# x transposed by channel tiles of four token tiles, with its loads and the weights' placed between the quarters of w_mod

## The chip, the cores and the metric

The kernel runs on one core of a Trainium2 chip. The core has five engines, each with its own queue that it works off in order: TensorE (PE, matrix products and transposes; its weight loads are shown apart as PEld), VectorE (DVE), ScalarE (ACT), GpSimd (POOL) and SyncE (SP, which here issues the DMAs). PE writes to PSUM, eight banks of 128 x 512 fp32 values; DVE and ACT read PSUM and the on-chip memory. Time is device microseconds (us) of one execution. Before the change: 1352.6 us, the median of three runs (1351.03 to 1353.95).

## What is computed

One layer of a diffusion transformer on 1024 latent tokens of width 1024, all in fp32: adaptive RMSNorm, one wide projection, windowed attention beside Fourier mixing, a gated merge, and a gated feed-forward with a short convolution. The part that matters here is the beginning, the modulated norm of x and the projection:

```python
def adaln(cvec, w_mod, b_mod):
    return jnp.split(jax.nn.silu(cvec) @ w_mod + b_mod, 6, axis=-1)
...
sh1, sc1, gt1, sh2, sc2, gt2 = [m[:, None] for m in adaln(c, w_mod[l], b_mod[l])]
...
h = modulate(rmsnorm(x, g_pre1[l]), sh1, sc1)
hc = modulate(rmsnorm(ctx, g_pre1[l]), csh1, csc1)
q, k, v, f, g_a, g_f = split_proj(h @ w_in[l])
```

`modulate(h, shift, scale)` is `h * (1 + scale) + shift`, one scale and one shift per channel. w_mod has 1024 rows and 6 x 1024 columns; the first 2048 columns give shift and scale of this norm, the other 4096 the four vectors needed later.

## The kernel before

**Precision.** A product of fp32 matrices is made of three products of a narrower type (`mm3`): each operand is split into a high part (a cast, on ACT) and a low part (source minus high part, on DVE); `split` does both. A matmul of 512 columns is issued three times, lines 85, 86 and 87.

**The projection.** h, transposed so that channels lie on the partitions, is the moving operand. It is cut in four: token half 1 or 2 by channel half 1 or 2, each of 4 channel tiles of 128 by 512 tokens: B11, B21, B12, B22. A Strassen-Winograd scheme (`wino`) multiplies a pair of column blocks of w_in with 7 products instead of 8: P1 to P7, with the operands B11, B21, B22 and the differences T1, T2, T3, T4n of the four pieces (`MOV`), and on the weights' side A11, A12, A22 and the sums S1 to S4 (`STA`). The first three pairs (j = 0 to 2: three pairs of gate columns) run in a hand-written order; items 0-2 are P1 of the three, 3-5 P2, 6-8 P5, 9-11 P6, 12-14 P7, 15 and 16 P4 and P3 of pair 0. `mm(i, ks)` issues the matmuls of item i for the channel tiles `ks` (all four: 12 matmuls), `conv(j, p)` splits the weight operand, `sums(j, s)` makes a sum on DVE, `evac(i)` copies or adds a result out of PSUM. One bank per pair holds P1, P6, P7 and P4 (X), one P5 and P3 (Y), one P2 (Z).

**The vectors.** The first 2048 columns of w_mod come in four quarters (`wm_stage(q)`, 8 loads of 256 KB each; quarter q holds shift and scale of channel tiles 2q and 2q + 1). `mod_rows(q, ks)` multiplies them with silu(c), `mod_copy` (DVE) takes the rows out of PSUM, `mod_turn` (PE, 8 tiny matmuls) turns them into columns, `mod_vec` (DVE) makes the scale `ax` and the shift `sx`. The other 4096 columns follow in groups of 512 (`ada_load`, `ada_rows`, `ada_copy`).

**x.** Eight token tiles of 128 tokens, each loaded as two halves of 512 channels (`x_load`). `x_square` sums squares on ACT, `x_norm` makes 1/rms of two tiles, `x_scale` scales. Then, for one token tile and one channel half, PE transposes four 128 x 128 blocks into one PSUM bank (`transpose8`, `turn`): the bank holds four channel tiles of one token tile. Scale and shift differ between channel tiles, so `affine` takes each block of 128 columns by itself, on ACT or DVE (`x_first` from PSUM; `x_second` from a raw copy, `x_raw`, for channel half 2 of the first four tiles). The splits (`hb_part`, `hb_puts`) go by token tile, too: pieces of 128 to 384 columns, since the operand lies in one buffer of 3 channel tiles and one of 1. The differences T1 to T4n are made per token tile over 512 columns.

**Order.** In the block under `tc.manual_schedule()` (from line 899) each engine runs its instructions in the order of the text. All loads of the block come first in it, so SP's queue starts with x tiles 0-3, the four quarters with A11 between the second and third, then the rest. `mm(3)` follows the split of B21, `mm(6)` that of T1, `mm(9)` that of T2, `mm(12)` that of T3, item 15 needs T4n and item 16 B22. From item 17 on `run` issues the items with their loads, splits and evacuations a fixed number of items ahead.

Of the kernel before, what the change touches and what calls it, by code (L numbers as in the profile page):

```python
# [13 lines left out]
ALU = mybir.AluOpType  # L14
# [26 lines left out]
def block_kernel(ctx: ExitStack, tc: tile.TileContext, t: dict, out: bass.AP, dbg: dict):  # L41
# [18 lines left out]
    def s(name, dtype=F):  # L60
        return spool.tile([P, 512], dtype, tag="s", name=name, bufs=40)
# [92 lines left out]
    def transpose8(xn, psf, name):  # L154

        res = []
        for kh in range(2):
            pt = psf(f"pt{name}{kh}")
            for k in range(4):
                nc.tensor.transpose(pt[:, k * P:(k + 1) * P], xn[kh][:, k * P:(k + 1) * P], ident)  # L160
            res.append(pt)
        return res
# [375 lines left out]
    def affine(out, src, kh, eng, ks):  # L538
        for k in ks:
            a, b = ax[:, 0, kh * 4 + k:kh * 4 + k + 1], sx[:, 0, kh * 4 + k:kh * 4 + k + 1]  # L540
            o, i = out[:, k * P:(k + 1) * P], src[:, k * P:(k + 1) * P]
            if eng is None:
                nc.scalar.activation(out=o, in_=i, func=AF.Identity, scale=a, bias=b)
            else:
                eng.tensor_scalar(out=o, in0=i, scalar1=a, scalar2=b, op0=ALU.mult, op1=ALU.add)

    def x_turn(tk):
        pt[tk] = transpose8(xs[tk], ps, f"x{tk}")
# [3 lines left out]
    def x_raw(tk):  # L552

        hraw[tk, 1] = s(f"hr{tk}1")
        copy(hraw[tk, 1], pt[tk][1])
# [343 lines left out]
    with tc.manual_schedule():  # L899
        for tk in range(4):  # L900
# [12 lines left out]
        pre(1, ("A12",))  # L913
# [12 lines left out]
        for tk in range(2):  # L926
            for i in range(2):
                x_scale(tk, i, nc.vector)
        x_turn(0)
        x_turn(1)  # L930
        x_norm(2)
        mod_rows(0, range(4))
        for tk in range(2, 4):
            for i in range(2):
                x_scale(tk, i, nc.vector)
        x_raw(0)
        x_raw(1)
        x_turn(2)
        x_turn(3)
        x_raw(2)  # L940
        x_raw(3)
# [24 lines left out]
        mod_rows(2, range(8))
        ada_load(1, range(KT))
        mm(0, range(2, 4))
        mod_copy(2)
        mod_turn(2)  # L970
        mm(1, range(2, 4))
        mod_vec(2)
        engs = (nc.vector, None, None, nc.vector)
        b21 = {c: hraw[c, 1] for c in (0, 1, 3, 2)}
        for c in range(4):
            x_second(c, (0, 1), engs[c])
        mod_rows(3, range(4))
        mm(2, range(2, 4))
        mod_rows(3, range(4, 8))
        ada_load(2, range(KT))  # L980
        hb_part(hb, "B21", b21, 0, 2)
        conv(0, "P2")
        mod_copy(3)
        mod_turn(3)
        x_square(4)
        x_square(5)
        mod_vec(3)

        def turn(tk, kh):
            p_ = ps(f"ptx{tk}{kh}")  # L990
            for k in range(4):
                nc.tensor.transpose(p_[:, k * P:(k + 1) * P], xs[tk][kh][:, k * P:(k + 1) * P], ident)
            pt.setdefault(tk, {})[kh] = p_
# [24 lines left out]
        for tk in (6, 7):
            turn(tk, 0)
        for tk in (6, 7):  # L1020
            x_first(tk, range(4), 0, alt_(tk))
        mm(5)
        ada_rows(0, 1)
        for c in range(4):
            t1(c)
        sums(0, "S1")
        hb_puts(hb, "T1", {c: hraw[c, 0] for c in range(4)})
        conv(0, "P5")
        ada_copy(0)
        ada_load(3, range(KT))  # L1030
        for tk in range(4, 8):
            x_scale(tk, 1, None)
        ada_rows(1, 0)
        ada_rows(1, 1)
        ada_copy(1)
        ada_load(4, range(KT))
        for tk in (4, 5):
            turn(tk, 1)
        for j in range(3):
            evac(j)  # L1040
        for j in range(3, 6):
            evac(j, True)
        sums(1, "S1")
        conv(1, "P5")
        for tk in (4, 5):
            x_first(tk, range(4), 1)
        mm(6)
        for tk in (6, 7):
            turn(tk, 1)
        sums(2, "S1")  # L1050
        conv(2, "P5")
        for tk in (6, 7):
            x_first(tk, range(4), 1)
        mm(7)
        ada_rows(2, 0)
        for j in range(3):
            sums(j, "S3")
            sums(j, "S2")
        conv(0, "P6")
        mm(8)  # L1060
        ada_rows(2, 1)
        for c in range(4):
            sub(hraw[c, 0], hraw[c + 4, 1], hraw[c, 0])
        hb_puts(hb, "T2", {c: hraw[c, 0] for c in range(4)})
# [24 lines left out]
        for c in range(4):  # L1089
            sub(hraw[c, 0], hraw[c, 1], hraw[c, 0])  # L1090
# [4 lines left out]
        hb_puts(hb, "T4n", {c: hraw[c, 0] for c in range(4)})  # L1095
        mm(13)
        mm(14)
        hb_puts(hb, "B22", {c: hraw[c + 4, 1] for c in range(4)})
# [1104 lines left out]
```

## Time and profile before

| | us |
|---|---|
| median of three runs | 1352.6 |
| the profiled execution | 1355.45 |
| its span, first to last instruction | 1353.7 |
| PE busy | 1276.7 |
| DVE busy | 1028.8 |
| ACT busy | 691.2 |
| POOL busy | 418.6 |

The profile is one execution, timed by the hardware. A line of the timeline gives start, duration, engine, source line, operation, result <- operands, shape and count, and in brackets how long the engine had been idle and what ended that. The same buffer names stand for all buffers of a kind: `hr` are the transposed tiles of x and the differences made of them, `hP`/`lP` the high and low part of a weight operand, `ptx` the transposes of x, `mr`, `mc` and `pm` the rows and columns of a quarter, `ar` and `ac` those of a group of 512. Line 68 is the helper of all DVE additions, line 80 the cast in `split`. A full fp32 matmul (rows, columns) appears as two records. The clock column is the share of TensorE's clock that was granted. Busy time of PE counts matmuls, also those at half clock.

### The profile page before, as it was taken

The numbers are of one execution on the slowest core, as the hardware profiler recorded it, in microseconds if no ns is written. First come the engines' busy times: TensorE is split into PE (matmuls) and PEld (weight loads), VectorE is DVE, ScalarE is ACT, GpSimd is POOL, SyncE is SP. The second block draws the span as 40 slices with busy tenths as digits, with TensorE's granted clock in tenths as the row PEclk, the third lists the DMA queues.
The fourth block names the chain that finished last, engine by engine and source line by source line (L and its number), as shares of the span: only waits on it lengthen the run. The fifth ranks groups of instructions, "written<-read, shape, count | busy, mean of one in ns | idle before, by whom it ended". The sixth has DMA issues, their size and how long they took to land.

```text
span 1353.7 us, 18460 instructions
## 1 busy us (share of the span) xinstructions
PE 1276.7 (94%) x5976; PEld 1027.9 (76%) x5976; DVE 1028.8 (76%) x1827; ACT 691.2 (51%) x1421; POOL 418.6 (31%) x317
## 2 busy tenths in 40 slices
PE   5899999999899999999999999999999988989896
PEld 3557877888888877778877788888888876878774
DVE  4687686975788995777889986776667687696977
ACT  5685345533667774344576544444445444443442
POOL 0000120200334333000005554445434356272754
PEclk9899999999999999999999999999999999999998
DMA  9986384514233444754213664444343569847563
GB/s 308 357 286 195 99 267 140 171 51 124 90 109 103 130 128 147 241 164 140 86 39 93 172 171 117 134 132 132 110 127 104 158 189 300 279 141 239 178 207 125
DMA packets 251125, 219.42 MB, mean 162 GB/s; under 512 B 14972, under 2 KB 204052, under 8 KB 251028
## 3 DMA queue, kind: packets, MB, share of 16 engines
q1 hardware_dynamic: 251028, 218.25, 52.2%
q8 instruction: 47, 0.77, 0.2%
q14 instruction: 50, 0.41, 0.1%
HBM read 159.20 MB, written 58.72 MB: 161 GB/s over the span
## 4 chain that ended last, share of the span: by engine, by line
PE 64%; DVE 20%; ACT 5%; DMA 5%; issue 4%; POOL 1%; SPq 0%; DVEq 0%; POOLq 0%; ACTq 0%
PE X_u L87 5%; PE X_u L85 5%; PE X_u L86 5%; PE Y_u L85 2%; PE Y_u L87 2%; PE Y_u L86 2%; PE X_g L85 2%; PE X_g L87 2%; PE X_g L86 2%; DVE p L1285 2%; PE X_d L85 2%; PE X_d L86 2%; PE X_d L87 2%; DVE pl L68 2%; DVE dT L68 2%
## 5 line engine op out<-in xcount | busy, mean ns | idle before, releaser
L68 DVE TENSOR_TENSOR lP_u<-A_u,hP_u 128x512 fp32r<-128x512 f32 x132 | 101.6, 778 | 48.0 <-ACT hP_u L303 46.4
L365 ACT COPY snP_u<-X_u 128x512 f32<-128x512 f32 x57 | 33.5, 588 | 138.3 <-PE X_u L87 130.5
L1305 POOL TENSOR_SCALAR p<-p,sm 128x640 f32<-128x640 f32 (+1 forms) x64 | 48.5, 780 | 91.6 <-PE pp L1310 40.0
L303 ACT CAST hP_u<-A_u 128x512 fp32r<-128x512 f32 x121 | 74.6, 619 | 0.1
L68 POOL TENSOR_TENSOR yd<-yd,snP_d 128x512 f32<-128x512 f32 x36 | 52.2, 1452 | 70.5 <-ACT snP_d L365 70.5
L68 POOL TENSOR_TENSOR A_u<-A_u,A_u 128x512 f32<-128x512 f32 x39 | 62.9, 1613 | 34.3 <-DVE lP_u L68 19.9
L365 ACT COPY snP_d<-X_d 128x512 f32<-128x512 f32 x48 | 28.1, 586 | 80.4 <-PE X_d L87 78.7
L68 POOL TENSOR_TENSOR A_u<-S_u,A_u 128x512 f32<-128x512 f32 x19 | 24.8, 1308 | 104.3 <-DVE lP_u L68 104.3
L80 ACT CAST ph<-pp 128x512 fp32r<-128x512 f32 x76 | 44.3, 585 | 22.5 <-PE pp L1310 21.2
L68 DVE TENSOR_TENSOR pl<-pp,ph 128x512 fp32r<-128x512 f32 x76 | 51.6, 681 | 2.5 <-ACT ph L80 2.1
L1299 ACT ACTIVATE p<-p,nm 128x640 f32<-128x640 f32 (+1 forms) x64 | 51.4, 803 | 0.7 <-DVE nm L1292 0.7
L68 DVE TENSOR_TENSOR lP_d<-rP_d,hP_d 128x384 fp32r<-128x384 f32 x48 | 42.3, 882 | 10.5 <-ACT hP_d L303 10.3
L1285 DVE CUSTOM_DVE_ANT_0 p<-ss,mask 128x640 f32<-128x640 f32 (+1 forms) x64 | 49.9, 781 | 0.0
L1310 PE MATMUL pp<-ident,p 128*128 128x128 f32 x304 | 46.7, 273 | 2.8 <-POOL p L1305 1.5
L2057 POOL MEMSET u<- 128x1 f32 x2 | 0.2, 99 | 153.4 <-DVE z L1630 149.0
L1710 DVE SCALAR_TENSOR_TENSOR tb<-u,vec,tb 128x1024 f32<-128x1024 f32 x22 | 40.9, 1860 | 6.8 <-ACT tb L1707 6.8
L1310 PEld LDWEIGHTS pp<-ident,p 128*128 128x128 f32 x304 | 37.2, 140 | 11.7 <-POOL p L1305 2.9
L68 POOL TENSOR_TENSOR S_u<-A_u,A_u 128x512 f32<-128x512 f32 x19 | 35.7, 1878 | 31.0 <-PE X_u L86 30.5
L68 POOL TENSOR_TENSOR shk<-shk,rope 128x512 f32<-128x512 f32 x2 | 3.3, 1626 | 134.8 <-DMA A_g<-in_w_in 128.9
L68 DVE TENSOR_TENSOR dB<-wd,dB 128x512 fp32r<-128x512 f32 x33 | 38.6, 1181 | 7.7 <-ACT dB L1781 7.7
L68 DVE TENSOR_TENSOR u<-Y_u,snP_u 128x512 f32<-128x512 f32 x22 | 15.2, 690 | 37.3 <-PE Y_u L87 37.3
L68 POOL TENSOR_TENSOR wd<-wd,wd 128x512 f32<-128x512 f32 x22 | 37.0, 1701 | 19.6 <-DVE dB L68 11.1
(898 smaller groups left out, 4561.2 us busy)
## 6 DMA issues: line engine op xcount, KB each, us to landing
A_u<-in_w_up SPq DMA_DIRECT2D x88, 256.0 KB, 3.9
wd<-in_w_down SPq DMA_DIRECT2D x55, 256.0 KB, 4.1
wa<-in_w_mod SPq DMA_DIRECT2D x36, 256.0 KB, 5.3
A_g<-in_w_in SPq DMA_DIRECT2D x32, 256.0 KB, 5.0
ws<-in_w_mod SPq DMA_DIRECT2D x30, 256.0 KB, 6.0
wm<-in_w_mod SPq DMA_DIRECT2D x30, 256.0 KB, 4.0
bP_d<-g_d0P SPq DMA_DIRECT2D x56, 128.0 KB, 3.2
x<-in_x SPq DMA_DIRECT2D x16, 256.0 KB, 5.7
```

The costliest lines, as they stand in the source:

```text
L68: return (eng or nc.vector).tensor_tensor(out=out, in0=a, in1=b, op=op)
L80: copy(hi, src)
L85: nc.tensor.matmul(ps, ah, bh, start=start, stop=False, skip_group_check=True)
L86: nc.tensor.matmul(ps, ah, bl, start=False, stop=False, skip_group_check=True)
L87: nc.tensor.matmul(ps, al, bh, start=False, stop=stop, skip_group_check=True)
L303: copy(st[j]["half", p][0], st[j][STA[p]])
L365: copy(d["s" + p], d["X"])
L1285: nc.vector.tensor_tensor_reduce(out=p_, in0=ssc[:, lo:768], in1=self.mk, op0=ALU.add, op1=ALU.max, scale=1.0, scalar=-3.0e38, accum_out=s ...
L1299: nc.scalar.activation(out=self.pt[g], in_=self.pt[g], func=AF.Exp, scale=SCALE, bias=self.m[:, g:g + 1], accum_out=self.sm[:, g:g + 1])
L1305: nc.gpsimd.tensor_scalar(out=self.pt[g], in0=self.pt[g], scalar1=self.sm[:, g:g + 1], scalar2=1.0, op0=ALU.mult, op1=ALU.mult)
L1310: nc.tensor.transpose(pp[:, g * P:(g + 1) * P], self.pt[g][:, j * P:(j + 1) * P], ident)
L1710: nc.vector.scalar_tensor_tensor(out=tb, in0=u[:, 0:1024], scalar=cw[0], in1=tb, op0=ALU.mult, op1=ALU.add)
```

## The change

- Transposes go by channel tile: `x_turn(half, k)` collects channel tile k of the four token tiles of one half in one bank, so that one scale and one shift hold for 512 columns. `x_mod` does them in one instruction, on ACT for even and on DVE for odd k; `x_put` splits one channel tile in one cast and one subtraction of 512 columns. The raw copies go. T1 to T4n are made per channel tile.
- The loads: A11 of pairs 0 and 1 stand between quarters 0 and 1, A11 of pair 2 and x tiles 4, 5 between 1 and 2, A12 of pairs 0, 1 and x tiles 6, 7 between 2 and 3.
- The order of the whole block is written anew.

```diff
+    def x_turn(half, k, cs=range(4)):
+        if cs[0] == 0:
+            pt[half, k] = ps(f"x{half}{k}")
+        for c in cs:
+            nc.tensor.transpose(pt[half, k][:, c * P:(c + 1) * P], xs[half * 4 + c][k // 4][:, k % 4 * P:(k % 4 + 1) * P], ident)
...
+    def x_mod(half, k, eng=None):
+        o, a, b = s(f"hr{half}{k}"), ax[:, 0, k:k + 1], sx[:, 0, k:k + 1]
+        if eng is None:
+            nc.scalar.activation(out=o, in_=pt[half, k], func=AF.Identity, scale=a, bias=b)
+        else:
+            eng.tensor_scalar(out=o, in0=pt[half, k], scalar1=a, scalar2=b, op0=ALU.mult, op1=ALU.add)
+        hraw[half, k] = o
+
+    def x_put(o, k, src):
+        split(mov[o][0][k], mov[o][1][k], src)
...
         wm_stage(0)
+        for j in range(2):
+            pre(j, ("A11",))
         wm_stage(1)
-        for j in range(3):
-            pre(j, ("A11",))
-        wm_stage(2)
-        wm_stage(3)
+        pre(2, ("A11",))
         x_load(4)
         x_load(5)
-        pre(0, ("A12",))
+        wm_stage(2)
+        for j in range(2):
+            pre(j, ("A12",))
         x_load(6)
         x_load(7)
-        pre(1, ("A12",))
+        wm_stage(3)
         pre(2, ("A12",))
...
+        conv(0, "P1")
         mod_copy(0)
         mod_turn(0)
         mod_vec(0)
...
+        mod_rows(1, range(4))
+        x_mod(0, 0)
+        x_mod(0, 1, V)
+        x_put("B11", 0, hraw[0, 0])
+        x_put("B11", 1, hraw[0, 1])
+        mm(0, range(2))
+        mod_rows(1, range(4, 8))
         ada_load(0, range(KT))
         mod_copy(1)
         conv(1, "P1")
+        mm(1, range(2))
         mod_turn(1)
         mod_vec(1)
+        x_mod(0, 2)
+        x_mod(0, 3, V)
         conv(2, "P1")
+        x_put("B11", 2, hraw[0, 2])
+        x_put("B11", 3, hraw[0, 3])
         mm(2, range(2))
+        x_square(4)
+        x_turn(0, 4)
+        x_turn(0, 5)
+        x_square(5)
+        mm(0, range(2, 4))
+        mod_rows(2, range(4))
...
+        mod_rows(2, range(4, 8))
...
         mod_turn(2)
         mod_vec(2)
+        x_mod(0, 4)
+        x_mod(0, 5, V)
         conv(0, "P2")
+        x_put("B21", 0, hraw[0, 4])
+        x_put("B21", 1, hraw[0, 5])
+        for j in range(3):
+            evac(j)
+        x_turn(0, 6)
+        x_turn(0, 7)
         x_square(6)
         x_square(7)
+        conv(1, "P2")
+        mm(3, range(2))
         x_norm(6)
         for tk in (6, 7):
+            x_scale(tk, 0, V)
+        mm(4, range(2))
+        mod_rows(3, range(8))
+        mod_copy(3)
+        ada_load(2, range(KT))
+        mod_turn(3)
+        mod_vec(3)
+        x_mod(0, 6)
+        x_mod(0, 7, V)
...
+        x_put("B21", 2, hraw[0, 6])
+        x_put("B21", 3, hraw[0, 7])
+        conv(2, "P2")
+        mm(3, range(2, 4))
+        def t1(k):
+            sub(hraw[0, k], hraw[1, k], hraw[0, k])
...
+        mm(4, range(2, 4))
+        sums(0, "S1")
+        for k in range(2):
+            t1(k)
+            x_put("T1", k, hraw[0, k])
+        for k in range(2, 4):
+            x_mod(1, k, V if k % 2 else None)
+        mm(5)
+        conv(0, "P5")
+        for k in range(2, 4):
+            t1(k)
+            x_put("T1", k, hraw[0, k])
         ada_rows(0, 0)
         ada_rows(0, 1)
+        mm(6)
+        for j in range(3, 6):
+            evac(j, True)
         ada_copy(0)
         ada_load(3, range(KT))
+        sums(1, "S1")
+        conv(1, "P5")
         for tk in range(4, 8):
+            x_scale(tk, 1, V if tk % 2 else None)
+        sums(0, "S3")
+        sums(0, "S2")
+        mm(7)
...
+        mm(8)
+        for j in range(1, 3):
             sums(j, "S3")
             sums(j, "S2")
+        for k in range(2):
+            sub(hraw[0, k], hraw[1, k + 4], hraw[0, k])
+            x_put("T2", k, hraw[0, k])
+        for k in range(6, 8):
+            x_mod(1, k, V if k % 2 else None)
         conv(0, "P6")
+        ada_rows(2, 0)
         ada_rows(2, 1)
+        for k in range(2, 4):
+            sub(hraw[0, k], hraw[1, k + 4], hraw[0, k])
+            x_put("T2", k, hraw[0, k])
         ada_copy(2)
         ada_load(5, range(KT))
+        mm(9)
+        conv(1, "P6")
+        conv(2, "P6")
         ada_rows(3, 0)
         ada_rows(3, 1)
         ada_copy(3)
         for j in range(4, 9):
             after(j)
+        mm(10)
         evac(9)
+        ada_rows(4, 0)
+        for k in range(4):
+            sub(hraw[1, k], hraw[1, k + 4], hraw[1, k])
+            x_put("T3", k, hraw[1, k])
         ada_rows(4, 1)
         mm(11)
         ada_rows(5, 0)
...
         mm(12)
         ada_rows(5, 1)
+        for k in range(4):
+            sub(hraw[0, k], hraw[0, k + 4], hraw[0, k])
+            x_put("T4n", k, hraw[0, k])
         mm(13)
         mm(14)
+        for k in range(4):
+            x_put("B22", k, hraw[1, k + 4])
```

More of the change, by code (lines that the diff above doesn't have):

```diff
@@ L925, in block_kernel @@
             x_square(tk)
[L926 to L930, printed above, removed]
+        for i in range(2):
+            for tk in range(2):
+                x_scale(tk, i, V)
+        for k in range(4):
+            x_turn(0, k, range(2))
         x_norm(2)
@@ L933, in block_kernel @@
         for tk in range(2, 4):
[L934 to L941, printed above, removed]
+            x_scale(tk, 0, V)
+        for k in range(4):
+            x_turn(0, k, range(2, 4))
         mod_rows(0, range(4, 8))
+        x_scale(2, 1, None)
+        x_scale(3, 1, None)
+        conv(0, "P1")
         mod_copy(0)
@@ L967, in block_kernel @@
+        x_turn(0, 4)
[3 more added lines that the diff above has]
+        mod_rows(2, range(4))
+        x_norm(4)
+        mm(1, range(2, 4))
+        mod_rows(2, range(4, 8))
+        for tk in (4, 5):
+            x_scale(tk, 0, V)
+        mod_copy(2)
         ada_load(1, range(KT))
-        mm(0, range(2, 4))
-        mod_copy(2)
+        mm(2, range(2, 4))
         mod_turn(2)
-        mm(1, range(2, 4))
         mod_vec(2)
-        engs = (nc.vector, None, None, nc.vector)
@@ L974, in block_kernel @@
[L974 to L981, printed above, removed]
-        conv(0, "P2")
[L983 to L993, printed above, removed]
@@ L1022, in block_kernel @@
-        mm(5)
-        ada_rows(0, 1)
[L1024 to L1028, printed above, removed]
+            x_scale(tk, 0, V)
+        mm(4, range(2))
[7 more added lines that the diff above has]
+        for k in range(2):
+            x_turn(1, k)
+        x_put("B21", 2, hraw[0, 6])
@@ new lines, in block_kernel @@
+        x_put("B21", 3, hraw[0, 7])
[4 more added lines that the diff above has]
+        for k in range(2):
+            x_mod(1, k, V if k else None)
+        for k in range(2, 4):
+            x_turn(1, k)
+        mm(4, range(2, 4))
+        sums(0, "S1")
+        for k in range(2):
+            t1(k)
+            x_put("T1", k, hraw[0, k])
+        for k in range(2, 4):
+            x_mod(1, k, V if k % 2 else None)
@@ L1033, in block_kernel @@
+        mm(7)
+        for k in range(4, 6):
+            x_turn(1, k)
+        sums(2, "S1")
+        conv(2, "P5")
         ada_rows(1, 0)
+        for k in range(4, 6):
+            x_mod(1, k, V if k % 2 else None)
         ada_rows(1, 1)
@@ L1094, in block_kernel @@
         ada_rows(5, 1)
-        hb_puts(hb, "T4n", {c: hraw[c, 0] for c in range(4)})
+        for k in range(4):
+            sub(hraw[0, k], hraw[0, k + 4], hraw[0, k])
+            x_put("T4n", k, hraw[0, k])
         mm(13)
         mm(14)
-        hb_puts(hb, "B22", {c: hraw[c + 4, 1] for c in range(4)})
+        for k in range(4):
+            x_put("B22", k, hraw[1, k + 4])
         ada_copy(5)
```

94 lines of the change are left out of this document (6 added, 88 removed).

## The prediction

> **What bounds the kernel now.** I read the page's busy shares first, then busy time by 20 us stretches, then TensorE's (PE's) waits, then its clock. The page's first section:
>
> ```profile
> PE 1276.7 (94%) x5976; PEld 1027.9 (76%) x5976; DVE 1028.8 (76%) x1827; ACT 691.2 (51%) x1421; POOL 418.6 (31%) x317
> ```
>
> PE is the bound. Where it isn't full the stretches tell (time, PE, weight loads, VectorE = DVE, ScalarE = ACT, POOL, clock, DMA share, GB/s):
>
> ```profile
> 20.00:40.00 20.00, 17.09 (x90) 10.63 (x83) 11.18 (x41) 7.82 (x24) 0.00 (x0) 0.83 1.10 349
> 40.00:60.00 20.00, 16.21 (x76) 10.33 (x74) 14.08 (x56) 15.03 (x45) 0.00 (x0) 0.83 1.06 339
> 60.00:80.00 20.00, 16.64 (x93) 10.95 (x86) 13.74 (x28) 16.05 (x40) 0.00 (x0) 0.91 1.05 394
> 80.00:100.00 20.00, 19.26 (x107) 10.47 (x107) 19.93 (x41) 15.62 (x37) 0.00 (x0) 1.00 0.65 220
> 100.00:120.00 20.00, 20.00 (x92) 15.59 (x92) 15.29 (x32) 14.97 (x35) 0.00 (x0) 1.00 0.68 211
> ```
>
> All that the change touches lies in the first 110 us. From 20 to 100 us PE idles 2.91 + 3.79 + 3.36 + 0.74 = 10.8 us; from 100 us it is full, so whatever delays PE before moves the end by as much. From 80 to 100 us DVE is full too. PE's longest waits from 20 us on, and its clock in stretches of 3.4 us (the first, the third and the last of five at half clock; the second and fourth follow the first and third without a gap):
>
> ```profile
> PE Z_g L85 <- ACT B21a L80: 2.1, 1, 2.1
> PE X_g L85 <- ACT hP_g L80: 1.9, 1, 1.9
> PE ptx L992 <- ACT ac L749: 1.6, 1, 1.6
> ```
> ```profile
> 28.00:31.40 3.40, 3.40 (x14) 3.02 (x13) 1.36 (x8) 0.47 (x2) 0.00 (x0) 0.50 1.10 349
> 51.90:55.30 3.40, 2.58 (x11) 2.27 (x11) 1.87 (x6) 3.22 (x9) 0.00 (x0) 0.50 0.99 353
> 72.40:75.80 3.40, 3.40 (x9) 2.64 (x8) 2.48 (x4) 2.10 (x6) 0.00 (x0) 0.51 1.05 397
> ```
>
> Each of the three waits is followed by such stretches, and all begin a multiple of 3.4 us apart. Five of them cost 5 x 1.7 = 8.5 us.
>
> [...]
>
> **The change, part by part.** *Wide pieces.* Durations by group and shape (count, busy, mean ns, idle before):
>
> ```profile
> L543 ACT ACTIVATE hr<-ptx,sx,ax 128x128 f32<-128x128 f32 x32 | 11.9, 475 | 10.0 <-DVE ax L596 6.7 <-PE ptx L992 3.2
> L545 DVE TENSOR_SCALAR hr<-ptx,ax,sx 128x128 f32<-128x128 f32 x16 | 5.5, 404 | 1.9 <-PE ptx L992 1.9
> L581 DVE COPY mc<-mr 128x512 f32<-128x512 f32 x4 | 2.8, 690 | 6.6 <-PE mr L577 6.6
> L555 ACT COPY hr<-ptx 128x512 f32<-128x512 f32 x4 | 2.4, 588 | 3.7 <-PE ptx L160 3.6
> L503 ACT ACTIVATE junk<-x 128x512 f32<-128x512 f32 x16 | 10.0, 628 | 0.4
> ```
>
> The 32 + 16 pieces from PSUM and 16 more from SBUF become 16 pieces of 512 columns, 8 on ACT, 8 on DVE; I take the nearest 512-column moves from PSUM, 0.6 and 0.69 us. ACT: 11.9 + 2.4 us (the raw copies go) become 8 x 0.6 = 4.8. DVE: 5.5 become 8 x 0.69 = 5.5, no gain. So ACT loses some 10 us of work, but it is half idle; that helps only where PE waits for it. The number of transposes, products and row groups on PE stays.
>
> [...]
>
> *The order on DVE and ACT.* Now an operand such as T4n is made by four subtractions in a row, then all casts, then all low parts. In the new order each channel tile goes through subtract (DVE), cast (ACT) and low part (DVE) before the next subtract. DVE runs in order, so it stands while ACT casts. Rows, start and duration:
>
> ```profile
> 62.82 2.49 DVE L68 TENSOR_TENSOR hr<-hr,hr 128x512 f32<-128x512 f32 x4
> 63.54 2.32 ACT L80 CAST T1a<-hr 128x384 fp32r<-128x384 f32 x4 [0.93 <-DVE hr L68]
> ```
> ```profile
> 76.98 0.66 ACT L80 CAST hP_g<-S_g 128x512 fp32r<-128x512 f32 x1
> 77.67 0.69 DVE L68 TENSOR_TENSOR lP_g<-S_g,hP_g 128x512 fp32r<-128x512 f32 x1 [2.03 <-ACT hP_g L80]
> 78.28 0.69 DVE L68 TENSOR_TENSOR A_g<-A_g,A_g 128x512 f32<-128x512 f32 x1
> ```
> ```profile
> 97.87 2.49 DVE L68 TENSOR_TENSOR hr<-hr,hr 128x512 f32<-128x512 f32 x4
> ```
> ```profile
> 102.16 0.90 DVE L68 TENSOR_TENSOR T4nb<-hr,T4nb 128x128 fp32r<-128x128 f32 x4
> ```
>
> Subtract to cast 0.72, cast to low part 0.69, low part to next subtract 0.61: 2.0 us a tile, 8.0 an operand, where T4n takes 97.87 to 103.06 = 5.2. T1, T2, T3 and T4n each hold DVE 2.8 us longer, where it is full already.
>
> *The requests.* x 0-3 and quarter 0 keep their place. Then (issue start, duration, count; and to landing):
>
> ```profile
> 5.84 11.12 SPq L480 DMA_DIRECT2D ws<-in_w_mod  x15
> ```
> ```profile
> ws<-in_w_mod SPq DMA_DIRECT2D x30, 256.0 KB, 6.0
> ```
>
> That is 0.74 us a request, 6.0 us to landing; moved requests only trade places. By count, the first two A11 tiles land at 18 and 19 us, quarter 1 is complete at 25, quarter 2 at 35, quarter 3 at 45 (two, four and ten requests later than now). Quarter 3 is wanted after 52 us below: covered by 7 us; without that cover it would cost its lateness.
>
> *The walk.* I place the new order, each engine in program order, with the steps above (DVE and ACT in a row 0.6 and 0.55), and PE's: a product (12 matmuls) 2.95 us, half of one 1.5; half of a row group 1.0, a quarter of w_mod 2.0; eight transposes 1.0. They are from these rows, which also bound the stages of now:
>
> ```profile
> 20.99 0.69 DVE L581 COPY mc<-mr 128x512 f32<-128x512 f32 x1 [3.84 <-PE mr L577]
> 26.63 0.50 PE L85 MATMUL X_g<-B11a,hP_g 128*128 128x512 f32 x1 [1.92 <-ACT hP_g L80]
> 44.93 0.69 DVE L581 COPY mc<-mr 128x512 f32<-128x512 f32 x1 [0.62 <-PE mr L577]
> 60.40 1.10 PE L992 MATMUL ptx<-ident,x 128*128 128x128 f32 x8
> 65.61 0.62 PE L745 MATMUL ar<-wa,sv 128*32 128x512 f32 x2
> 83.94 0.62 PE L745 MATMUL ar<-wa,sv 128*32 128x512 f32 x2
> 87.76 0.89 DVE L68 TENSOR_TENSOR T2b<-hr,T2b 128x128 fp32r<-128x128 f32 x4
> 90.59 1.06 PE L745 MATMUL ar<-wa,sv 128*32 128x512 f32 x8
> 95.54 0.50 PE L85 MATMUL X_g<-T2a,hP_g 128*128 128x512 f32 x1
> 98.49 1.06 PE L745 MATMUL ar<-wa,sv 128*32 128x512 f32 x8
> 102.43 0.62 PE L745 MATMUL ar<-wa,sv 128*32 128x512 f32 x2
> ```
>
> For each stage I compare what PE loses (idle and half clock), that is elapsed time less this work.
>
> 1. To mod_turn(2). A11 lands before quarter 0 is summed; conv(0)'s low part ends at 19.5 and mod_copy(0) follows it, 1.5 us earlier than now; the first product starts near 23, not 26.6. But quarter 1 ends at 25, conv(1)'s low part stands behind mod_copy(1), and PE waits about 0.8 for it and 1.7 us for conv(2), enough for one or two half-clock stretches. What now is done at 44.8, less 3.0 us that the new order hasn't done yet (8 transposes, quarter 3), is 41.8; I get 42.9. **Cost 1** (-1.5 to 2.5).
> 2. To the end of mm(5). B21's first two casts end on ACT at 45.6; then evac(0..2) (to 47.3) and the squares of tiles 6 and 7 (4 x 0.75, to 50.3) stand in front of conv(1, "P2"), which mm(4) needs, and mod_rows(3) is queued behind mm(4) on PE. PE does half of mm(3) by 47.1, stands until 50.9, then runs at half clock. Vectors 3 come at 58.8, B21's last low parts at 61, mm(5) ends at 67.1: 24.2 less 14.8 of work, 9.4 lost. Now: 44.8 to 65.6 less 12.9, 7.9. **Cost 1.5** (-2 to 4).
> 3. To the end of mm(8). T1, in two pairs from 62.9 on, ends at 72; then evac(3..5) and sums(1) (4 x 0.6) stand on DVE in front of conv(1, "P5"): mm(6) ends at 72.7, mm(7) starts at 75.3, and a half-clock stretch follows. End 86.9: 19.8 less 14.9, 4.9 lost. Now 18.3 less 14.9, 3.4. **Cost 1.5** (-1 to 3).
> 4. To the end of mm(9). DVE from 84 on: half of T2 (4 us), a wide piece, conv(0, "P6") with the S4 it triggers, half of T2: last low part about 94, now 88.65. mm(9) ends at 94.5; 7.6 less 4.9, 2.7 lost. Now 6.65 less 5.95, 0.7. **Cost 2** (0.5 to 3).
> 5. To the end of mm(12). On ACT ada_copy(3) waits for row group 3, which PE now takes after mm(9) (to 96.5); sigmoids, evac(9) and T3's casts queue behind it. T3 starts at 100.6, ends at 108, with conv("P7") behind; PE is through the row groups at 105.4 and waits until 107.7. End 110.9: 16.4 less 13.9, 2.5 lost; now 11.84 less 11.85, none. **Cost 2.5** (0 to 4).
> 6. To the end of mm(15). T4n runs 109.6 to 117.5, B22 and the split of P4 behind it to 120.8; PE is through mm(14) at 117.6. Now that split ends at 107.0, 2 us before mm(15):
>
> ```profile
> 106.31 0.69 DVE L68 TENSOR_TENSOR lP_g<-A_g,hP_g 128x512 fp32r<-128x512 f32 x1
> ```
> ```profile
> 109.01 0.39 PE L85 MATMUL X_g<-T4na,hP_g 128*128 128x512 f32 x1
> ```
>
> **Cost 3** (0 to 5).
>
> Sum 1 + 1.5 + 1.5 + 2 + 2.5 + 3 = **11.5 us**. The profiled execution took 1355.45 us (span 1353.7 and 1.75 around it), 2.85 over the median; 1355.45 + 11.5 = 1366.9 there, 1352.6 + 11.5 = **1364 us** at the median. The low ends add up to -4, the high ends to 21.5.
>
> [...]
>
> **Rivals.**
> *The cheaper pieces set the end (faster).* Stages 1 and 2 now hold four of the five half-clock stretches. The two longest waits name ACT, which loses 10 us of work; if the first product's lead of 3 us lasts and the gaps before 28 and 52 us close, 4 x 1.7 = 6.8 us go: 1345.8. It decides if PE shows no wait over 1.5 us before mm(5) and T2 to T4n come no later for PE than now. Against it: ACT's order in stage 2, and a full DVE from 80 us.
> *Even.* Stages 1 to 3 gain the 6.8 us, stages 4 to 6 lose 7.5: 1353.3.
> *Far slower.* The waits in stages 4 to 6 each fall so that a half-clock stretch follows (3 x 1.7), or shared buffers are freed later: 1369 to 1374. Waits of 2 us did this three times; from 80 to 120 us the clock is full now.
> *The requests help nothing.* DMA is at 349 GB/s to 40 us, and x and A11 arrive earlier only by what the quarters lose; then stage 1 costs 2.5, 1365.5, inside the forecast.
>
> **How the numbers follow.** About 0.2% (2.7 us) is what a measurement of this kernel can tell from no change. Chances: the forecast and its smaller relatives (3 to 17 us slower) 0.63, far slower 0.10, even 0.11, faster 0.16. So slower 0.73, same 0.11, faster 0.16. The range 1350 to 1371 leaves out most of "faster" and the end of "far slower", 0.2 together.
>
> **What would show it.** Right: mm(0) near 23 us; a PE wait of 3 to 4 us before mm(4) whose releaser is the cast of hP, with the squares just before it on ACT; DVE rows of hr and T2, T3, T4n alternating singly, each low part with 0.6 us idle on its cast; PE waits on T2, on T3 or P7, on T4n or P4 between 88 and 121 us, where there is one of 0.7 now. Wrong: four subtractions in a row as before, T2 complete by 89 us, or PE full from 88 us on; stages 4 to 6 then cost nothing and the sign turns on stages 1 and 2. A half-clock stretch more or less shifts all by 1.7 us.

## The result, and the profile after

The changed kernel takes 1369.4 us (median of 4 runs, 1368.0 to 1370.8), the kernel before beside it 1352.1: 17.2 us slower, ratio 1.0126, 95% interval [1.0109, 1.0144]. The forecast was 1364, 11.5 slower, with a range of 1350 to 1371. The profiled executions stand 14.2 us apart (spans 1367.9 and 1353.7); that of before was itself 3.3 us over its median, that of after 0.5, which is most of the difference from 17.2.

The busy shares of after, the first section of its page:

```profile
PE 1283.4 (94%) x5976; PEld 1029.0 (75%) x5976; DVE 1026.0 (75%) x1775; ACT 677.3 (50%) x1349; POOL 417.6 (31%) x317
```

DVE and ACT have fewer instructions than before (1775 for 1827, 1349 for 1421) and less work, and yet the kernel is slower. The stretches of 20 us, in the columns of the prediction:

```profile
20.00:40.00 20.00, 17.13 (x73) 10.53 (x74) 9.41 (x31) 7.76 (x17) 0.00 (x0) 0.74 1.09 353
40.00:60.00 20.00, 15.04 (x67) 7.97 (x66) 7.31 (x22) 7.28 (x17) 0.00 (x0) 0.74 1.04 334
60.00:80.00 20.00, 16.82 (x79) 11.42 (x79) 15.25 (x30) 9.12 (x15) 0.00 (x0) 0.89 1.01 368
80.00:100.00 20.00, 17.27 (x98) 9.48 (x97) 15.20 (x24) 7.16 (x12) 0.00 (x0) 0.94 0.39 133
100.00:120.00 20.00, 17.44 (x81) 10.21 (x82) 11.56 (x19) 11.53 (x20) 0.00 (x0) 0.91 0.56 174
```

Look at the last two rows. Before, PE was busy for 19.26 and 20.00 us of them at full clock; now for 17.27 and 17.44 at 0.94 and 0.91. DVE, 19.93 us busy from 80 to 100 before, is down to 15.20, and ACT from 15.62 to 7.16: all three have time to spare, so they wait for each other. PE's longest waits (20 to 140 us: total, number, longest) say for whom:

```profile
PE X_g L85 <- ACT hP_g L80: 4.4, 2, 2.5
PE Y_g L85 <- ACT hP_g L80: 2.3, 1, 2.3
PE Z_g L85 <- ACT hP_g L80: 2.3, 1, 2.3
PE pm L582 <- DVE mc L575: 2.2, 2, 1.3
PE ar L739 <- ACT hr L551: 1.8, 1, 1.8
PE Z_g L85 <- ACT B21a L80: 1.5, 1, 1.5
PE X_g L85 <- ACT snP_g L293: 1.2, 1, 1.2
```

In time order, by the stages of the prediction's walk: an X_g wait of 1.9 in stage 1; two Z_g waits in stage 2, of 1.5 before mm(3) and of 2.3 before mm(4); Y_g in stage 3, before mm(7); ar before stage 4's products; the X_g wait of 2.5 in stage 5, before mm(12); the last one in stage 6, before mm(15). The pm waits lie in front of the turns of vectors. ACT's rows in stage 2 and VectorE's while T4n is made show the two patterns behind them:

```profile
46.42 1.14 ACT L80 CAST B21a<-hr 128x512 fp32r<-128x512 f32 x2
47.46 1.55 ACT L293 COPY snP_g<-X_g 128x512 f32<-128x512 f32 x3
48.89 0.65 ACT L503 ACTIVATE junk<-x 128x512 f32<-128x512 f32 x1
...
51.80 0.60 ACT L80 CAST hP_g<-A_g 128x512 fp32r<-128x512 f32 x1
```

```profile
113.07 0.68 DVE L68 TENSOR_TENSOR hr<-hr,hr 128x512 f32<-128x512 f32 x1
114.44 0.69 DVE L68 TENSOR_TENSOR T4na<-hr,T4na 128x512 fp32r<-128x512 f32 x1 [0.69 <-ACT T4na L80]
115.05 0.68 DVE L68 TENSOR_TENSOR hr<-hr,hr 128x512 f32<-128x512 f32 x1
...
120.38 0.69 DVE L68 TENSOR_TENSOR T4nb<-hr,T4nb 128x512 fp32r<-128x512 f32 x1 [0.69 <-ACT T4nb L80]
```

First pattern: three evacuations and the squares of tiles 6 and 7 stand on ACT from 47.5 to 51.8 ahead of the cast that mm(4) needs. Second: subtract, 0.69 us idle on ACT's cast, low part, next subtract, 1.98 us a tile; T4n takes 113.07 to 121.07, 8.0 us, for 5.2 before.

### The profile page after: what moved, and what is told of

Read it like the earlier page. It is cut to its first block, busy times and chain, and to the rows that moved or that the text cites. A ratio compares the mean times of both kernels' runs of the same rounds, so it can differ in the third digit from the quotient of the medians.

```text
span 1367.9 us, 18327 instructions
## 1 busy us (share of the span) xinstructions
PE 1283.4 (94%) x5976; PEld 1029.0 (75%) x5976; DVE 1026.0 (75%) x1775; ACT 677.3 (50%) x1349; POOL 417.6 (31%) x317
## 4 chain that ended last, share of the span: by engine, by line
PE 61%; DVE 19%; DMA 7%; ACT 6%; issue 5%; POOL 1%; SPq 1%; DVEq 0%; POOLq 0%; ACTq 0%
PE X_u L87 5%; PE X_u L85 5%; PE X_u L86 5%; PE Y_u L85 3%; PE Y_u L86 2%; PE Y_u L87 2%; PE X_d L85 2%; DVE p L1287 2%; PE X_d L86 2%; PE X_d L87 2%; DMA ws<-in_w_mod 2%; DVE pl L68 2%; PE X_g L85 1%; PE X_g L86 1%; PE X_g L87 1%
## 5 line engine op out<-in xcount | busy, mean ns | idle before, releaser
L1307 POOL TENSOR_SCALAR p<-p,sm 128x640 f32<-128x640 f32 (+1 forms) x64 | 48.3, 774 | 91.8 <-PE pp L1312 35.3
L303 ACT CAST hP_u<-A_u 128x512 fp32r<-128x512 f32 x121 | 74.6, 619 | 0.1
L68 POOL TENSOR_TENSOR wd<-wd,wd 128x512 f32<-128x512 f32 x22 | 37.0, 1700 | 20.4 <-DVE dB L68 11.4
```

The lines of the kernel that those rows point to most:

```text
L68: return (eng or nc.vector).tensor_tensor(out=out, in0=a, in1=b, op=op)
L303: copy(st[j]["half", p][0], st[j][STA[p]])
L1307: nc.gpsimd.tensor_scalar(out=self.pt[g], in0=self.pt[g], scalar1=self.sm[:, g:g + 1], scalar2=1.0, op0=ALU.mult, op1=ALU.mult)
```

## The experiments

Theory A: the loss comes from the order of instructions on DVE and ACT, above all from the differences that alternate between the two. Theory B: it comes from the order of the requests. Theory C: it lies in the new layout, its wide pieces or its shared banks. The versions ran in three sessions, the first two on one chip and the third on another, each beside the kernel before; there it took 1354.0 (first four versions), 1354.1 (next four) and 1353.7 us (last three), and "over before" below is the difference of the medians of one session. By the intervals a version's distance from before is known to about 1.3 us where it ran ten times, and to 2 or 2.5 us where it ran four times, so a difference between two such distances is known to some 2 to 3.5 us.

| version | us | over before | ratio, 95% interval |
|---|---|---|---|
| the change | 1369.4 | +17.2 | 1.0126 [1.0109, 1.0144] |
| all differences grouped | 1355.9 | +1.9 | 1.0014 [1.0004, 1.0023] |
| only T1, T2 grouped | 1363.6 | +10.0 | 1.0067 [1.0048, 1.0085] |
| only T3, T4n grouped | 1363.4 | +9.3 | 1.0071 [1.0054, 1.0088] |
| conv(1, "P2") first | 1366.3 | +12.3 | 1.0091 [1.0073, 1.0109] |
| both | 1352.7 | -1.3 | 0.9985 [0.9976, 0.9995] |
| both, old requests | 1359.0 | +4.9 | 1.0044 [1.0028, 1.0061] |
| before, new requests | 1356.2 | +2.2 | 1.0017 [1.0007, 1.0026] |
| before, differences alternating | 1365.2 | +11.1 | 1.0087 [1.0072, 1.0102] |
| the change, PE's waits filled | 1366.6 | +12.9 | 1.0090 [1.0073, 1.0107] |
| both, early splits ahead | 1345.4 | -8.7 | 0.9939 [0.9924, 0.9953] |
| the same, narrow pieces | 1353.1 | -0.5 | 0.9992 [0.9982, 1.0001] |

**Differences grouped.** In the changed kernel the subtractions run first, then the splits (T1 and T2 in their pairs, T3 and T4n all four):

```diff
         for k in range(4):
             sub(hraw[0, k], hraw[0, k + 4], hraw[0, k])
+        for k in range(4):
             x_put("T4n", k, hraw[0, k])
```

> The changed kernel with T1 to T4n made as before: the subtractions of a group first (pairs for T1 and T2, four for T3 and T4n), then their casts and low parts; still by channel tiles of 512 columns. Theory A (the order on DVE and ACT costs the time): DVE no longer stands 0.7 us before each low part; T3 takes about 4 us less, T4n 3, the pairs 1.3 each; PE's waits before the T3 product (2.5) and the T4n product (1.2) shrink; 6 to 8 us faster than the changed kernel, 1361 to 1364. Theory B (the order of the requests) and theory C (the wide pieces): within 2 us of the changed kernel, 1367.5 to 1371.

It came out at 1.9 us over before, where the change has 17.2: 15.3 us back, about twice what was expected. The stretch from 100 to 120 us:

```profile
100.00:120.00 20.00, 20.00 (x95) 14.90 (x95) 17.44 (x29) 15.69 (x31) 0.00 (x0) 1.00 0.75 225
```

PE is full again, and DVE does 17.44 us of work in a stretch where it did 11.56. No instruction was added or taken out, so some 15 of the 17 us go with this order.

**conv(1, "P2") first.** In the changed kernel, that split goes ahead of evac(0..2) and the squares of tiles 6 and 7.

```diff
         x_put("B21", 1, hraw[0, 5])
+        conv(1, "P2")
         for j in range(3):
             evac(j)
...
         x_square(7)
-        conv(1, "P2")
```

> The changed kernel with the split of P2 of pair 1 moved ahead of evac(0..2) and the squares of tiles 6 and 7 on ACT. Theory A: PE's wait of 2.3 us before mm(4) goes, and with it most of the half clock from 48 to 59 us; 3 to 5 us faster than the changed kernel, 1364 to 1366.5. Theories B and C: no change, since PE would wait at the next place for the late quarter 3 or the same vectors; 1368 to 1371.

Against before it gave 5 us back (12.3 for 17.2), as expected; the Z_g wait on the cast of hP is gone from its waits, and those of stages 3 to 5 are as long as in the change. Its profile is of the slowest of its four executions (1370.3 us, the other three 1365.8 to 1366.4), in which the wait before mm(15) is 2.7 us instead of 1.2 and half clock follows it (the granted clock is 0.91 from 120 to 140 us, 1.00 in after); of the gain it shows the part in stage 2.

**Both.**

> Both edits of the two runs before. Theory A: they lie in different stretches (45 to 60 us, 65 to 125 us) and add up, 9 to 13 us faster than the changed kernel, 1356 to 1360. B and C: within 3 us of it.

Better than expected: 1.3 us below the kernel before. Alone the two edits gave 15.3 and 4.9 us against before, together they give 18.5. So the two orders cost more than the 17.2, and what is left of the change without them is worth the 1.3 us.

**The requests alone.** The kernel before, with the changed kernel's order of requests and nothing else of it.

> The kernel before with the changed order of the requests alone. Quarter 1 is complete at 25 us instead of 23.3, quarter 3 at 45.7 instead of 38; PE takes quarter 1 from 22.8 and quarter 3 from 41.1 to 44.8. Theory A: waits of about 1.5 and 1 to 2 us, perhaps one half-clock stretch more: 2 to 5 us slower than before, 1354 to 1357. Theory B: most of the 17 us, over 1362. If the rest of the early order hides them: 1352.

2.2 us slower, with an interval that excludes no change, but far from 17: B falls as the main cause.

**The order alone, in the old layout.** The kernel before, with T1 to T4n made token tile by token tile:

```diff
+        sums(0, "S1")
         for c in range(4):
             t1(c)
-        sums(0, "S1")
-        hb_puts(hb, "T1", {c: hraw[c, 0] for c in range(4)})
+            hb_puts(hb, "T1", {c: hraw[c, 0]})
```

and so for T2, T3 and T4n. The subtractions of T4n also move to the place of its splits, behind what `lead` issues, and the sum S1 of pair 0 now comes ahead of T1.

> The kernel before, in its old layout by token tiles and with its old requests; of the change only the order on VectorE is taken: each of T1, T2, T3 and T4n is made tile by tile (subtract, cast, low part) where four subtractions ran first. Theory A (the alternating order makes VectorE stand on ScalarE's casts, and that is most of the change's loss): 6 to 12 us over the kernel before, with PE waits on T2, T3 or T4n between 80 and 115 us where before there is one of 0.7. Theory C (the loss belongs to the new layout, its wide pieces or its shared PSUM banks): within 2 us of before.

11.1 us slower: the order costs most of this without the new layout, too, where grouping gave 15.3 back in the new one. (Part of the 11.1 can come from the moved subtractions and sum; that wasn't tried apart.) DVE's rows for T4n in this kernel show the same stop on ACT's cast:

```profile
107.36 0.69 DVE L68 TENSOR_TENSOR hr<-hr,hr 128x512 f32<-128x512 f32 x1
108.63 0.56 DVE L68 TENSOR_TENSOR T4na<-hr,T4na 128x384 fp32r<-128x384 f32 x1 [0.58 <-ACT T4na L80]
...
109.31 0.68 DVE L68 TENSOR_TENSOR hr<-hr,hr 128x512 f32<-128x512 f32 x1
```

and its PE waits have T2 at the head:

```profile
PE X_g L85 <- ACT T2a L80: 3.8, 1, 3.8
```

**T3 and T4n alone, T1 and T2 alone.** Two versions of the changed kernel with one half of the grouping each.

> The changed kernel with only T3 and T4n made in the old way (four subtractions first, then the splits); T1 and T2 alternate as in the change. Grouping all four gave 13.4 us back. Theory A with my stage costs (T3 2.5 and T4n 3 us, and half-clock stretches that follow their waits): 5 to 9 us below the changed kernel, so 1360 to 1364, and no PE wait on T3, T4n or on the products behind them after 100 us. Rival (nearly all comes from T1 and T2, since delays there pass down the order on VectorE): less than 3 us below the changed kernel.

> The changed kernel with only T1 and T2 grouped (in each pair both subtractions first, then both splits); T3 and T4n alternate as in the change. Grouping all four gave 13.4 us back, T3 and T4n alone 6.0. Theory A (the four operands' losses add up): 7 to 8 us below the changed kernel, so near 1362, with the waits ahead of the products of T3 and T4n still there. Rival (T1 and T2 only delay what T3 and T4n then lose again, so the parts don't add up): less than 4 us or over 10.

Against before they stand at +9.3 (T3 and T4n grouped) and +10.0 (T1 and T2); from 17.2 that is 7.9 and 7.2 back, together 15.1, where all four gave 15.3. Within the noise the parts add up, so a delay of T1 or T2 isn't swallowed by the next wait. With T3 and T4n grouped PE shows no wait after 98 us; with T1 and T2 alone grouped it still waits 2.5 us ahead of mm(12) and 1.1 ahead of mm(15), nearly as in the change. (One of the four executions of the T1 and T2 version took 1359.2 us, the other three 1363.5 to 1363.9; its profile is of the first.)

**Old requests in the mended version.**

```diff
         wm_stage(0)
-        for j in range(2):
+        wm_stage(1)
+        for j in range(3):
             pre(j, ("A11",))
-        wm_stage(1)
-        pre(2, ("A11",))
+        wm_stage(2)
+        wm_stage(3)
...
```

> The version with both orders mended (differences grouped; conv(1, P2) ahead of evac(0..2) and the squares), now with the requests in the order of the kernel before. Theory A (the new request order is worth next to nothing in either layout; in the old layout it cost 2.2 us): within 3 us of the mended version, either side, 1350 to 1356. Theory B (the new layout needs the new requests, since its first products come earlier): 4 to 8 us above it, with PE waits for A11 or x before 35 us.

6.2 us above the mended version, by the differences from before: theory B's size. The wait isn't directly for A11 or x, though; the head of PE's waits tells what it is for:

```profile
PE pm L582 <- DVE mc L575: 8.8, 2, 7.2
```

```profile
24.62 0.69 DVE L68 TENSOR_TENSOR lP_g<-A_g,hP_g 128x512 fp32r<-128x512 f32 x1 [8.62 <-ACT hP_g L80]
25.23 0.68 DVE L575 COPY mc<-mr 128x512 f32<-128x512 f32 x1
```

The changed text has conv(0, "P1") ahead of mod_copy(0) on DVE. With the old requests A11(0) is late, DVE stands in front of its low part until 24.6, and mod_copy(0), whose rows PE had finished at 18.8, stands behind it. So the new requests aren't a gain by themselves (+2.2 in the old layout); the new order of the splits needs them.

**Early splits ahead.** On top of both: conv(1, "P1") ahead of mod_copy(1), conv(2, "P1") ahead of mod_turn(1), conv(0, "P2"), conv(1, "P2") and the squares of tile 6 ahead of mod_turn(2), the squares of tile 7 ahead of evac(0..2), and two transposes of the second half ahead of the pieces of vectors 3. In short:

```diff
+        conv(1, "P1")
         mod_copy(1)
-        conv(1, "P1")
...
+        conv(2, "P1")
         mod_turn(1)
...
         ada_load(1, range(KT))
+        conv(0, "P2")
+        conv(1, "P2")
+        x_square(6)
         mm(2, range(2, 4))
         mod_turn(2)
```

> The mended version with the early stages reordered too: the splits of A11(1) and A11(2) ahead of mod_copy(1) and of the x pieces that wait for vectors 1; the splits of A12(0), A12(1) and the squares of tile 6 while ScalarE is idle before vectors 2; two transposes of the second half ahead of the pieces of vectors 3. Theory A (PE's waits before 60 us, 8 us of them in the mended version, come from the order on ScalarE and VectorE): PE's waits of 1.9, 0.8 and 1.5 us go, and with them a half-clock stretch or two: 3 to 6 us below the mended version, 1346 to 1350, below both kernels. Rival (the last quarter's landing at 45.3 us, or VectorE, which is 91% busy from 60 to 80 us, takes the place of these waits): less than 2 us.

1345.4 us, 8.7 below the kernel before, ratio 0.9939 [0.9924, 0.9953]: it beats both kernels, and by more than expected (7.4 us below the mended version against before). Its stretches:

```profile
20.00:40.00 20.00, 19.14 (x108) 11.85 (x108) 12.26 (x41) 11.10 (x24) 0.00 (x0) 1.00 1.09 353
40.00:60.00 20.00, 17.28 (x88) 11.42 (x92) 15.00 (x35) 11.03 (x22) 0.00 (x0) 0.91 1.11 356
60.00:80.00 20.00, 18.95 (x112) 11.48 (x108) 18.04 (x30) 9.48 (x16) 0.00 (x0) 1.00 1.05 396
80.00:100.00 20.00, 20.00 (x110) 12.37 (x103) 17.68 (x30) 17.16 (x32) 0.00 (x0) 1.00 0.89 300
```

Against after, PE is busy 9 us more in these 80 us, and the clock, 0.74 to 0.94 there, is full but for one stretch. The X_g waits of 1.9 and 0.8 us are gone; the one on B21's cast is 1.2 us instead of 1.5. DVE at 18 of 20 us from 60 us on didn't take the place of the waits. Whether the kernel before, in its old layout, would gain as much from such an order of its early splits wasn't tried.

**Narrow pieces.** The early version, each piece of 512 columns cut into four of 128:

```diff
-            nc.scalar.activation(out=o, in_=pt[half, k], func=AF.Identity, scale=a, bias=b)
...
+        for c in range(4):
+            cs = slice(c * P, (c + 1) * P)
+            if eng is None:
+                nc.scalar.activation(out=o[:, cs], in_=pt[half, k][:, cs], func=AF.Identity, scale=a, bias=b)
...
```

> The early version (1345.4 us; differences grouped, early splits ahead), with every scale-and-shift piece of 512 columns cut again into four of 128, as wide as in the kernel before; layout, splits and order stay. By the rows of before (475 ns on ScalarE, 404 on VectorE) a pair of pieces takes some 1.9 instead of 0.8 us. Theory A (the width is worth little because ScalarE has room; only the pieces right behind vectors 0 to 3 lie on PE's path): 2 to 5 us slower, 1347 to 1350, with longer PE waits on casts of B11 and B21 before 55 us. Theory C (wide pieces are the gain of the new layout): over 6 us slower. Rival (hidden): within 1 us.

8.2 us slower against before (-0.5 for -8.7), by the two intervals some 5 to 9.5 us: more than the 2 to 5 that theory A gave the width, and near C's "over 6", though not surely over it. The pieces of both kernels, first the early version, then the narrow one:

```profile
L553 DVE TENSOR_SCALAR hr<-x,ax,sx 128x512 f32<-128x512 f32 x8 | 6.4, 805 | 0.0
L551 ACT ACTIVATE hr<-x,sx,ax 128x512 f32<-128x512 f32 x8 | 6.2, 772 | 10.6 <-DVE ax L590 10.6
```

```profile
L553 ACT ACTIVATE hr<-x,sx,ax 128x128 f32<-128x128 f32 x32 | 12.0, 454 | 12.7 <-DVE ax L592 11.2 <-PE x L543 1.5
L555 DVE TENSOR_SCALAR hr<-x,ax,sx 128x128 f32<-128x128 f32 x32 | 10.9, 405 | 0.0
```

The narrow pieces add 5.8 us to ACT and 4.5 to DVE. Two of PE's waits, the first of which is 0.8 us in the early version and the second missing there:

```profile
PE ar L741 <- ACT hr L553: 2.2, 1, 2.2
...
PE Y_g L85 <- ACT hP_g L80: 1.2, 1, 1.2
```

Neither engine is the bound by its share; but a piece stands in front of the split of its channel tile, and where PE waits for that split the longer time of its four pieces is added to the wait; this is argued from the rows, not tried. How the 8.2 divide between longer waits and half clock (0.92 from 80 to 100 us, 1.00 with wide pieces) wasn't tried.

In these rows four narrow pieces take 2.0 times one wide piece on DVE (4 x 405 ns for 805), 2.4 times on ACT (4 x 454 for 772).

**PE's waits filled.** The changed kernel, with products that nobody reads put into four of PE's idle stretches:

```diff
+        def fill(n, name):
+            pd, b = ps(f"fill{name}"), mov["B11"][0][0]
+            for i in range(n):
+                nc.tensor.matmul(pd, b[:, :P], b, start=i == 0, stop=i == n - 1, skip_group_check=True)
...
+        fill(6, 0)
         mm(3, range(2))
+        fill(8, 1)
...
+        fill(10, 2)
         mm(7)
...
+        fill(10, 3)
         mm(12)
```

> The changed kernel with 34 added products in four of TensorE's idle stretches (6 ahead of mm(3), 8 ahead of mm(4), 10 ahead of mm(7), 10 ahead of mm(12)); nobody reads their sums. The waits stay as long, but PE isn't idle in them. If idle stretches of 1.5 to 2.5 us bring on the half clock (my theory), the half-clock stretches behind those places, some 16 us in the profile of the changed kernel between 48 and 117 us, mostly go, and the kernel gets 3 to 7 us faster, 1362 to 1366. If the half clock has another cause, the added work makes it 0 to 2 us slower.

4.2 us back against before (12.9 for 17.2), though PE has 34 products more to do; at 1366.6 us it lies just above the 1362 to 1366 that were expected. The same three stretches in after and in this kernel:

```profile
46.00:58.00 12.00, 8.32 (x28) 3.85 (x28) 4.72 (x14) 6.51 (x17) 0.00 (x0) 0.59 0.99 323
74.60:83.00 8.40, 5.96 (x18) 3.84 (x17) 6.94 (x12) 2.81 (x5) 0.00 (x0) 0.80 0.67 231
108.60:117.00 8.40, 5.84 (x24) 2.98 (x20) 6.27 (x10) 4.92 (x10) 0.00 (x0) 0.80 0.44 123
```

```profile
46.00:58.00 12.00, 9.35 (x48) 5.22 (x46) 5.25 (x15) 6.27 (x16) 0.00 (x0) 1.00 1.11 355
74.60:83.00 8.40, 8.40 (x52) 5.40 (x51) 6.89 (x12) 3.75 (x6) 0.00 (x0) 1.00 0.52 188
108.60:117.00 8.40, 8.01 (x26) 6.12 (x26) 5.66 (x10) 4.16 (x8) 0.00 (x0) 0.62 0.04 12
```

In the first two the clock goes from 0.59 and 0.80 to 1.00: with PE kept busy no half clock came there, although 1.3 us of the wait before mm(4) was left unfilled. (One stretch follows the unfilled waits of 0.9 and 0.7 us that end at 56.9 and 58.7: the clock is 0.50 from 61.0 to 62.7 us.) In the third the filling failed and shows the opposite:

```profile
PE fill L899 <- ACT ac L743: 4.0, 1, 4.0
```

The added products had themselves to wait, for a free bank as it seems (the copy of a row group ended the wait), PE stood for 4.0 us, and the half clock came, worse than in after (0.62 for 0.80). This run shows that the first two idle stretches brought on the half clock behind them (0.59 and 0.80 with them, 1.00 without); it doesn't show how long one must be. In the version with conv(1, "P2") first, the wait before mm(12) is as long as in after, and no half clock follows it:

```profile
108.23 0.50 PE L85 MATMUL X_g<-T3a,hP_g 128*128 128x512 f32 x1 [2.49 <-ACT hP_g L80]
```

There the granted clock is 1.00 from 100 to 120 us.

A wait as short as 2.3 us cost clock here: half clock followed the one before mm(7) in after (0.50 from 78.9 to 82.3 us), and with products in its place the clock stayed full (1.00 from 74.6 to 83).

## Why the prediction was right, and where its sizes were off

The direction and the main steps held; the size was short by 5.7 us, inside the range. Most of the signs came, too: mm(0) began at 23.9 us, the rows of hr and of T2, T3 and T4n alternate singly with 0.69 us idle before each low part, and PE waited before the products of T2, T3 and T4n. The wait before mm(4) was 2.3 us where 3 to 4 were forecast. The rows that begin right where stages 1 to 6 end, in order (stage 1: the last row group's turn, with its duration):

```profile
43.74 0.95 PE L582 MATMUL pm<-sel,mc 128*128 128x2 f32 x8
...
70.64 0.64 PE L739 MATMUL ar<-wa,sv 128*32 128x512 f32 x4
...
91.42 1.07 PE L739 MATMUL ar<-wa,sv 128*32 128x512 f32 x8 [1.77 <-ACT hr L551]
...
98.01 1.06 PE L739 MATMUL ar<-wa,sv 128*32 128x512 f32 x8
...
115.71 0.97 PE L739 MATMUL ar<-wa,sv 128*32 128x512 f32 x2
...
126.82 0.39 PE L85 MATMUL Y_g<-B22a,hP_g 128*128 128x512 f32 x1
```

The third starts after 1.77 us of waiting, so stage 3 ended at 89.65.

| stage, to | walk | measured | late by | of it in this stage |
|---|---|---|---|---|
| 1, mod_turn(2) | 42.9 | 44.7 | 1.8 | +1.8 |
| 2, mm(5) | 67.1 | 70.6 | 3.5 | +1.7 |
| 3, mm(8) | 86.9 | 89.65 | 2.75 | -0.75 |
| 4, mm(9) | 94.5 | 98.0 | 3.5 | +0.75 |
| 5, mm(12) | 110.9 | 115.7 | 4.8 | +1.3 |
| 6, mm(15) | 123.3 | 126.8 | 3.5 | -1.3 |

The 123.3 is the walk's 117.6 for mm(14), plus 3 lost, plus 2.7 for mm(15). So the walk was 3.5 us early at its end: the row that begins at 126.82 began at 111.73 before, so the sum of 11.5 should have been 15.1, and the spans differ by 14.2. The rest up to 17.2 is not a step of the sum: the profiled execution of before stood 3.3 us over the median of the runs shown with the result. It is luck that stages 3 and 6 came 2 us cheaper and took back a part of what stages 1, 2, 4 and 5 cost too much.

The walk's stages stand against before and don't give the price of an order by itself. From the end of mm(5) to that of mm(15) before takes 46.1 us, the change 56.2 and the grouped version 44.2. Walk and trace agree that stages 3 to 6 cost 9 us against before (beside 1 us of work moved into them), but the alternating order alone costs 12 there, since before itself loses some 4 us in these stages that the grouped version mostly doesn't.

- *Stage 1, 1.8 us more.* The waits before conv(1)'s low part and conv(2)'s split were about those of the walk (0.8 and 1.9 us, 0.8 and 1.7 there). The term that was too small is the half clock: where the walk had "one or two half-clock stretches" of 3.4 us, there were three, the last two in a row:

```profile
21.20:24.60 3.40, 3.40 (x11) 1.14 (x12) 2.60 (x9) 2.44 (x4) 0.00 (x0) 0.55 1.11 354
31.40:38.20 6.80, 6.10 (x19) 5.04 (x20) 3.93 (x13) 4.68 (x13) 0.00 (x0) 0.52 1.11 348
```

- *Stage 2, 1.7 us more.* The cast of hP came behind evacuations and squares, as forecast (51.8 for 50.3). But mm(3) itself stood 1.5 us for B21's cast, so the wait before mm(4) was 2.3 us and not 3.8, and the half clock had begun before it:

```profile
47.09 0.49 PE L85 MATMUL Z_g<-B21a,hP_g 128*128 128x512 f32 x1 [1.48 <-ACT B21a L80]
...
48.27 0.63 PE L87 MATMUL Z_g<-B21a,lP_g 128*128 128x512 f32 x1
```

At clock 1.00 such a row takes 0.39 us (in after the one that starts at 69.64), not 0.63. The half clock lasted some 10 us from 48.3 on (0.51 from 48.4 to 58.6), and another stretch came at 62 us (0.51 from 61.9 to 65.3), behind waits of 0.9 and 0.7 us; the walk has half clock in this stage after mm(4)'s wait alone. Moving that split and nothing else gave 5 us, more than this stage's cost of 1.5, which stands against a stage of before with waits and half clock of its own (0.50 from 51.9 to 58.7 us).
- *Stage 3, right.* The wait before mm(7) was 2.3 us (2.6 in the walk), and a half-clock stretch followed (0.50 from 78.9 to 82.3 us).
- *Stage 4, right in size, partly by another wait.* PE stood 1.77 us in front of row group 2, which the walk didn't have: the group's bank comes free with the piece x_mod(1, 6), which stands on ACT behind T2's second cast, and that waits for DVE. That the bank is shared is read from the row that ended the wait, not tried. It is the alternating order again; with the differences grouped this wait is 0.9.
- *Stage 5, 1.3 us more.* T3's casts came behind ada_copy(3), the sigmoids and evac(9), and PE waited 2.5 us (2.3 in the walk); the half clock after it (0.52 from 112.9 to 116.3 us, the 0.80 above) wasn't in the walk. This is a piece of the rival "far slower".
- *Stage 6, 1.3 us less.* T4n took the 8.0 us of the forecast, but PE came late itself and so waited 1.2 us instead of 3. The wait names the copy that evacuates P7 of pair 0 out of bank X (ACT, 123.33 to 123.91), in which P4 is then made: the walk had waited for P4's split, which stands just ahead of this copy on ACT, and both stand behind the casts of T4n and B22.
- *The price of a wide piece was wrong.* The text took 0.6 and 0.69 us, from plain moves of 512 columns. With a scale and a shift a piece takes 0.775 us on ACT and 0.805 on DVE in after (the rows of the early version above are nearly the same), so the two groups cost 6.2 and 6.4 us instead of 4.8 and 5.5. The sum also left out the 16 old pieces from the on-chip memory, in the rows of before:

```profile
L543 ACT ACTIVATE hr<-hr,sx,ax 128x128 f32<-128x128 f32 x8 | 3.3, 483 | 6.4 <-DVE ax L596 6.4
L545 DVE TENSOR_SCALAR hr<-hr,ax,sx 128x128 f32<-128x128 f32 x8 | 2.2, 342 | 0.0
```

With them ACT lost 11.4 us (17.6 to 6.2) where the text had some 10, and DVE 1.3 (7.7 to 6.4) where it had none. The two errors work against each other, and no stage of the walk is made of these totals.

Of the rivals, "the cheaper pieces set the end" didn't come true in the change, but the width of the pieces does count where the waits are gone: there the narrow pieces cost 8.2 us. That the early version came out at 1345.4, near the 1345.8 of that rival, is chance: the rival's figure stands for four half-clock stretches and no change of order. "The requests help nothing" is right for the old layout (2.2 us slower), and wrong for the new one, where, as far as the trace tells, it is the split queued ahead of mod_copy(0) that needs them. "Far slower" (1369 to 1374) is where the median fell; its mechanism, half clock behind each new wait of stages 4 to 6, shows in stage 5 alone (0.52 from 112.9 to 116.3 us; 1.00 from 89.6 to 112.6 and from 120 to 140).

## What to carry to other kernels

A chain subtract (DVE), cast (ACT), low part (DVE) that is written tile by tile made DVE, which worked in order, stand 0.69 us once a tile here; written as all subtractions, then all splits, it took the same instructions and 15 us less of 1369. Before an engine that waits is called idle, look at what is queued in front of the awaited instruction: one split moved ahead of copies and squares was worth 5 us, and a split whose load was late, queued ahead of a copy whose data was ready, cost 6. A layout that saves work on engines that aren't the bound can still pay (some 8 us for the wide pieces, in the version with the mended order): judged with its first order, this one looked like a loss of 17.

## What was not expected of the hardware

- Half clock came behind idle stretches of TensorE of 2.5 us and less (in after no wait of PE is longer from 20 us on), and stayed away in two places where they were filled with work that nobody needs: these went from clock 0.59 and 0.80 to 1.00, and the kernel, with 34 products more, got 4 us faster. The length of a wait doesn't decide alone: in after half clock followed waits of 1.5 and 0.3 us close together (0.51 from 48.4 to 58.6 us) and of 0.9 and 0.7 us (0.51 from 61.9 to 65.3), and none followed the 1.77 us before 91.4 us (1.00 from 89.6 to 99.8); with conv(1, "P2") first none followed 2.49 us (1.00 from 100 to 120). What decides wasn't tried.
- A scale and shift of 512 columns out of PSUM takes 0.775 us on ACT and 0.805 on DVE in after, more than a plain move of the same size there (0.588 and 0.690 in the rows of before).
